# Mean of ReLU over rows: 126 rows a partition with two blocks of 128 rows, and a last row in pieces of 576, 192 and 256 columns

## The chip, the cores and the metric

One NeuronCore of a Trainium2 chip. The metric is the device time of one execution in microseconds (us); every run counted here was in the fast state at a granted clock of 1.00. ACT is ScalarE, DVE VectorE, POOL GpSimd, SP SyncE, which issues all transfers.

## The reference

```python
x: float32 [32, 512, 1024]           # 67.11 MB
return np.mean(np.maximum(x, 0), axis=-1)   # float32 [32, 512]
```

It is 16,384 rows of 1024 floats, each reduced to one float. Every byte of x is read once and used once.

## The kernel before

128 rows form a first block (one row a partition). The other 16,256 rows are laid out 127 consecutive rows a partition and read in tiles of 16 rows (8.39 MB, three buffers), then in pieces of 7, 4, 2 and 1 rows, and the last row in three column pieces.

```python
xfirst, xmain = xf[:P, :], xf[P:, :]
J = J - 1                                            # 127
xr = xmain.rearrange("(p j) d -> p j d", p=P, j=J)
NB, BUFS = 16, 3
row_pieces = [7, 4, 2, 1]
col_pieces = [512, 256, 256]
# ... SyncE issues the loads in order; each has its own semaphore
for t in range(full):
    buf_free(t)
    if t == 0:
        load(-1, row0[:, :], xfirst)
    load(t, bufs[t % BUFS][:, :, :], xr[:, t * NB:(t + 1) * NB, :])
# ... then row_pieces and col_pieces
# compute: even rows of a partition on ACT, odd ones on DVE, each with an accumulator
done = (dve_row if j % 2 else act_row)(nc, xt[:, k, :], sums[:, j:j + 1])
# ... the end, on the last row (n_done counts the signals so far):
nc.scalar.wait_ge(loaded[i + 1], 16)
act_row(nc, last[:, :512], last[:, D:D + 1]).then_inc(act, 1)
nc.vector.wait_ge(loaded[i + 2], 16)
dve_row(nc, last[:, 512:768], last[:, D + 1:D + 2]).then_inc(dve, 1)
nc.vector.wait_ge(act, n_done + 1)
nc.vector.wait_ge(dve, n_done + 1)
nc.vector.wait_ge(loaded[i + 3], 16)
nc.vector.scalar_tensor_tensor(                      # the final operation: takes the last 256
    out=last[:, 768:], in0=last[:, 768:], scalar=0.0,  # columns and both partial sums
    in1=scale[:, :], op0=ALU.max, op1=ALU.mult, accum_out=res[:, J - 1:J],
).then_inc(dve, 1)
nc.sync.wait_ge(pool, 2)
nc.sync.wait_ge(dve, n_done + 2)
nc.sync.dma_start(out=outr, in_=res[:, :]).then_inc(stored, 16)
```

The two partial sums sit in two columns behind the 256 data columns, so the final operation reads 258 elements. In the builds an instruction carries one wait of its own, and further waits are put into a separate semaphore instruction ahead of it.

Of the kernel before, what the change touches and what calls it, by code (L numbers as in the profile page):

```python
# [9 lines left out]
ACT = mybir.ActivationFunctionType  # L10


def act_row(nc, src, acc):

    return nc.scalar.activation(out=src, in_=src, func=ACT.Relu, accum_out=acc)  # L15


def dve_row(nc, src, acc, init=None):

    return nc.vector.tensor_scalar(  # L20
        out=src, in0=src, scalar1=0.0, scalar2=init,
        op0=ALU.max, op1=ALU.add, accum_out=acc,
    )


def issue_ahead_of_entry_barrier(nc, n):


    entry = nc.cur_f.blocks[0].instructions
    for _ in range(n):  # L30
        body, load = next(
            (block.instructions, k)
            for block in nc.cur_f.blocks[1:]
            for k, ins in enumerate(block.instructions)
            if ins.opcode == "DMACopy"
        )
        first = body[load]
        assert first.engine == mybir.EngineType.SP and not first.sync_info.on_wait
        assert all(i.opcode in ("Drain", "EventSemaphore") or i.engine != first.engine for i in body[:load])
        del body[load]  # L40
        at = next(k for k, i in enumerate(entry) if i.engine == first.engine and i.opcode == "Drain")
        entry.insert(at, first)


@with_exitstack
def kernel(
    ctx: ExitStack,
    tc: tile.TileContext,
    x: bass.AP,
    out: bass.AP,  # L50
):


    tc.close()
    tc.compile()  # L55

    nc = tc.nc
    P = nc.NUM_PARTITIONS
    xf = x.flatten_outer_dims()
    R, D = xf.shape  # L60
    assert R % P == 0
    J = R // P
    inv = 1.0 / D

    xfirst, xmain = xf[:P, :], xf[P:, :]
    outfirst, outmain = out.flatten()[:P], out.flatten()[P:]
    J = J - 1
    xr = xmain.rearrange("(p j) d -> p j d", p=P, j=J)
    outr = outmain.rearrange("(p j) -> p j", p=P, j=J)

    NB = 16
    BUFS = 3
    full = J // NB

    row_pieces = [7, 4, 2, 1]
    assert full * NB + sum(row_pieces) + 1 == J
    col_pieces = [512, 256, 256]
    assert sum(col_pieces) == D

    def sbuf(name, *shape):  # L80
        return ctx.enter_context(nc.sbuf_tensor(name, list(shape), F32))

    bufs = [sbuf(f"rows{b}", P, NB, D) for b in range(BUFS)]
    sums, res, part = sbuf("sums", P, J), sbuf("res", P, J), sbuf("part", P, 2)


    last = sbuf("last", P, D + 2)
    scale = sbuf("scale", P, D // 4 + 2)

    row0, mean0, turned0 = sbuf("row0", P, D), sbuf("mean0", P, 32), sbuf("turned0", P, 32)  # L90


    loaded = [nc.alloc_semaphore(f"loaded{i}") for i in range(full + len(row_pieces) + len(col_pieces) + 1)]
    act, dve, pool = (nc.alloc_semaphore(n) for n in ("act", "dve", "pool"))
    first = nc.alloc_semaphore("first")
    stored = nc.alloc_semaphore("stored")



    hinted = (nc.scalar, nc.vector)  # L100
    flag = nc.alloc_registers("flag", engines=[e.engine for e in hinted])
    nc.regs_mov(flag, 1)
    nc.br("rows_begin", engines=mybir.ALL_ENGINES)
    body = ctx.enter_context(nc.body("rows_begin", valid_engines=mybir.ALL_ENGINES))
    hints = [e.mark_branch_hint_location() for e in hinted]


    def load(i, dst, src):
        nc.sync.dma_start(out=dst, in_=src).then_inc(loaded[i], 16)

    def buf_free(t):

        if t >= BUFS:
            nc.sync.wait_ge(act, t - BUFS + 1)
            nc.sync.wait_ge(dve, t - BUFS + 1)

    for t in range(full):
        buf_free(t)
        if t == 0:
            load(-1, row0[:, :], xfirst)  # L120
        load(t, bufs[t % BUFS][:, :, :], xr[:, t * NB:(t + 1) * NB, :])
        if t == BUFS:

            nc.sync.wait_ge(first, 2)
            nc.sync.dma_start(
                out=outfirst.rearrange("(q i) -> q i", i=32), in_=turned0[0:P:32, :],
            ).then_inc(stored, 16)
    j0 = full * NB
    buf_free(full)
    xt = bufs[full % BUFS]  # L130
    lo, i = 0, full
    for n in row_pieces:
        load(i, xt[:, lo:lo + n, :], xr[:, j0 + lo:j0 + lo + n, :])
        lo, i = lo + n, i + 1
    c = 0
    for w in col_pieces:
        load(i, last[:, c:c + w], xr[:, J - 1, c:c + w])
        c, i = c + w, i + 1


    nc.gpsimd.memset(mean0[:, :], 0.0)  # L141
    nc.gpsimd.memset(scale[:, :], inv).then_inc(pool, 1)  # L142

    def rows(i, xt, lo, n, j0):
        nc.scalar.wait_ge(loaded[i], 16)
        nc.vector.wait_ge(loaded[i], 16)
        for k in range(lo, lo + n):
            j = j0 + k
            done = (dve_row if j % 2 else act_row)(nc, xt[:, k, :], sums[:, j:j + 1])
            if k >= lo + n - 2:  # L150
                done.then_inc(dve if j % 2 else act, 1)

    def finish(after, lo, hi):

        nc.gpsimd.wait_ge(act, after)
        nc.gpsimd.wait_ge(dve, after)
        nc.gpsimd.tensor_scalar(  # L157
            out=res[:, lo:hi], in0=sums[:, lo:hi], scalar1=inv, scalar2=0.0, op0=ALU.mult, op1=ALU.add,
        )

    nc.scalar.wait_ge(pool, 1)
    nc.vector.wait_ge(pool, 1)
    nc.scalar.wait_ge(loaded[-1], 16)
    nc.scalar.activation(  # L164
        out=row0[:, :], in_=row0[:, :], func=ACT.Relu, scale=inv, accum_out=mean0[:, 0:1],
    ).then_inc(first, 1)
    nc.vector.wait_ge(first, 1)
    nc.vector.transpose(turned0[:, :], mean0[:, :]).then_inc(first, 1)  # L168
    for t in range(full):
        rows(t, bufs[t % BUFS], 0, NB, t * NB)  # L170
    finish(full, 0, j0)
    lo, i = 0, full
    for n in row_pieces[:-1]:
        rows(i, xt, lo, n, j0)
        lo, i = lo + n, i + 1
    finish(i, j0, j0 + lo)


    prev = xt[:, lo, :]
    nc.scalar.wait_ge(loaded[i], 16)  # L180
    act_row(nc, prev[:, :448], part[:, 0:1]).then_inc(act, 1)
    nc.vector.wait_ge(loaded[i], 16)
    dve_row(nc, prev[:, 448:], part[:, 1:2]).then_inc(dve, 1)
    n_done = i + 1
    nc.gpsimd.wait_ge(act, n_done)
    nc.gpsimd.wait_ge(dve, n_done)
    nc.gpsimd.tensor_scalar(  # L187
        out=res[:, J - 2:J - 1], in0=part[:, 0:1], scalar1=part[:, 1:2], scalar2=inv, op0=ALU.add, op1=ALU.mult,
    ).then_inc(pool, 1)
    nc.scalar.wait_ge(loaded[i + 1], 16)  # L190
    act_row(nc, last[:, :512], last[:, D:D + 1]).then_inc(act, 1)
    nc.vector.wait_ge(loaded[i + 2], 16)
    dve_row(nc, last[:, 512:768], last[:, D + 1:D + 2]).then_inc(dve, 1)
    nc.vector.wait_ge(act, n_done + 1)
    nc.vector.wait_ge(dve, n_done + 1)
    nc.vector.wait_ge(loaded[i + 3], 16)
    nc.vector.scalar_tensor_tensor(  # L197
        out=last[:, 768:], in0=last[:, 768:], scalar=0.0, in1=scale[:, :], op0=ALU.max, op1=ALU.mult,
        accum_out=res[:, J - 1:J],
    ).then_inc(dve, 1)  # L200


    nc.sync.wait_ge(pool, 2)
    nc.sync.wait_ge(dve, n_done + 2)
    nc.sync.dma_start(out=outr, in_=res[:, :]).then_inc(stored, 16)

    used = [s.num for s in (*loaded, act, dve, pool, first)]
    assert used == list(range(used[0], used[0] + len(used)))
    nc.sync.sem_clear(range(used[0], used[-1] + 1))
    nc.sync.wait_ge(stored, 32).then_inc(stored, -32)  # L210

    for e, hint in zip(hinted, hints):
        e.br_lt(flag, 1, on_true="rows_begin", on_false="rows_end").branch_hint(hint)
    nc.br("rows_end", engines=[e for e in mybir.ALL_ENGINES if e not in (h.engine for h in hinted)])
    nc.switch_bb("rows_end")

    issue_ahead_of_entry_barrier(nc, 2)
# [30 lines left out]
```

## Time and profile before

| what | before |
|---|---|
| time, median of the first 3 runs (lowest to highest) | 161.46 us (161.40 to 161.55) |
| span of the profile | 160.2 us |
| DVE / ACT busy | 46% / 44% |
| DMA queue's share of 16 engines | 97.7% |
| last load complete, by the trace's semaphore records | 157.82 us |
| final store issued / complete | 158.57 / 160.21 us |

The lines are in the prediction. Read them in this order: busy shares (no engine is full, so something else sets the time), the DMA queue's share (it is full), the table of stretches (the rate is even), and last the timeline of the end, the only place where compute is not hidden by loads.

### The profile page before, as it was taken

How to read it: one execution, taken by the hardware profiler on the slowest of the kernel's cores; microseconds unless marked ns; L12 is line 12 of the kernel's file. 1: busy time of each engine (PE TensorE's matmuls, PEld its weight loads, DVE VectorE, ACT ScalarE, POOL GpSimd, SP SyncE). 2: the span in 40 equal slices, each digit the busy share in tenths (PEclk: the TensorE clock that was granted, in tenths of full speed). 3: DMA queues.
4: the chain of work that ended last, by engine and by line, in shares of the span. 5: the costliest groups of instructions: out<-in, count | busy, mean ns of one | idle time of the engine just before them, and what ended most of it. 6: DMA issues, size and time to landing. Idle time of an engine off the chain costs nothing. (4 is left out here: it accounts for less than half of the span.)

```text
span 160.2 us, 347 instructions
## 1 busy us (share of the span) xinstructions
DVE 73.3 (46%) x131; ACT 70.4 (44%) x133; POOL 1.3 (1%) x9
## 2 busy tenths in 40 slices
DVE  0000029900498006960079500993009920299984
ACT  1400029800496006950079300991009900299983
POOL 1000000000000000000000000000000000000001
DMA  9969969979989899699699699699699797998992
GB/s 393 507 278 523 507 278 523 442 344 523 409 376 523 360 425 524 294 491 523 262 524 523 262 523 524 262 523 523 262 524 458 327 523 327 425 451 367 419 412 102
DMA packets 2312, 67.18 MB, mean 419 GB/s; under 512 B 392, under 2 KB 648, under 8 KB 1032
## 3 DMA queue, kind: packets, MB, share of 16 engines
q1 hardware_dynamic: 2312, 67.18, 97.7%
HBM read 67.11 MB, written 0.07 MB: 419 GB/s over the span
## 5 line engine op out<-in xcount | busy, mean ns | idle before, releaser
L20 DVE TENSOR_SCALAR_CACHE_REDUCE rows<-rows 128x1024 f32<-128x1024 f32 (+1 forms) x63 | 72.1, 1208 | 78.9 <-DMA rows<-in_x_dram 78.7
L15 ACT ACTIVATE rows<-rows 128x1024 f32<-128x1024 f32 x64 | 66.2, 1035 | 84.1 <-DMA rows<-in_x_dram 83.9
L15 ACT ACTIVATION_READ_ACCUMULATOR rows<-rows 128x1 f32 x64 | 11.9, 186 | 0.0
L20 DVE DVE_READ_ACCUMULATOR rows<-rows 128x1 f32 x63 | 5.2, 82 | 0.0
L168 DVE STREAM_TRANSPOSE turned<-mean 128x32 f32<-128x32 f32 x1 | 0.2, 213 | 5.9 <-ACT row L164 5.9
L164 ACT ACT_TABLE_LOAD x1 | 1.3, 1283 | 3.3 <-DMA row<-in_x_dram 3.3
L157 POOL TENSOR_SCALAR res<-sums 128x112 f32<-128x112 f32 (+1 forms) x2 | 0.5, 250 | 154.0 <-DVE rows L20 154.0
L164 ACT ACTIVATE row<-row 128x1024 f32<-128x1024 f32 x1 | 1.1, 1056 | 0.0
L15 ACT ACTIVATE last<-last 128x512 f32<-128x512 f32 x1 | 0.6, 630 | 0.0
L20 DVE TENSOR_SCALAR_CACHE_REDUCE last<-last 128x256 f32<-128x256 f32 x1 | 0.4, 420 | 0.3 <-DMA last<-in_x_dram 0.3
L197 DVE SCALAR_TENSOR_TENSOR last<-last,scale 128x258 f32<-128x258 f32 x1 | 0.4, 428 | 0.1
L142 POOL MEMSET scale<- 128x258 f32 x1 | 0.3, 314 | 0.0
L187 POOL TENSOR_SCALAR res<-part 128x1 f32<-128x1 f32 x1 | 0.3, 267 | 0.6 <-DVE rows L20 0.6
L164 ACT ACTIVATION_READ_ACCUMULATOR row<-row 128x1 f32 x1 | 0.2, 186 | 0.0
L15 ACT ACTIVATION_READ_ACCUMULATOR last<-last 128x1 f32 x1 | 0.2, 186 | 0.0
L141 POOL MEMSET mean<- 128x32 f32 x1 | 0.1, 126 | 1.5 <-POOLq L55 1.5
L232 POOL MEMSET const-uint8-127<- 128x1 uint8 x1 | 0.1, 103 | 0.0
L232 POOL MEMSET const-bfloat16-1.0<- 128x1 bf16 x1 | 0.1, 102 | 0.0
L232 POOL MEMSET const-float32-0.0<- 128x1 f32 x1 | 0.1, 99 | 0.2 <-issue 0.2
L232 POOL MEMSET const-float32-1.0<- 128x1 f32 x1 | 0.1, 99 | 0.0
L20 DVE DVE_READ_ACCUMULATOR last<-last 128x1 f32 x1 | 0.1, 83 | 0.0
L197 DVE DVE_READ_ACCUMULATOR last<-last,scale 128x1 f32 x1 | 0.1, 82 | 0.0
## 6 DMA issues: line engine op xcount, KB each, us to landing
rows<-in_x_dram SPq DMA_DIRECT2D x1, 3584.0 KB, 38.1
rows<-in_x_dram SPq DMA_DIRECT2D x1, 2048.0 KB, 42.6
rows<-in_x_dram SPq DMA_DIRECT2D x1, 1024.0 KB, 44.7
row<-in_x_dram SPq DMA_DIRECT2D x1, 512.0 KB, 3.3
rows<-in_x_dram SPq DMA_DIRECT2D x1, 512.0 KB, 45.4
last<-in_x_dram SPq DMA_DIRECT2D x1, 256.0 KB, 45.6
last<-in_x_dram SPq DMA_DIRECT2D x2, 128.0 KB, 45.4
rows<-in_x_dram SPq DMA_DIRECT2D x7, 48.8
```

The lines of the kernel that those rows point to most:

```text
L15: return nc.scalar.activation(out=src, in_=src, func=ACT.Relu, accum_out=acc)
L20: return nc.vector.tensor_scalar(out=src, in0=src, scalar1=0.0, scalar2=init, op0=ALU.max, op1=ALU.add, accum_out=acc,)
L141: nc.gpsimd.memset(mean0[:, :], 0.0)
L142: nc.gpsimd.memset(scale[:, :], inv).then_inc(pool, 1)
L157: nc.gpsimd.tensor_scalar(out=res[:, lo:hi], in0=sums[:, lo:hi], scalar1=inv, scalar2=0.0, op0=ALU.mult, op1=ALU.add,)
L164: nc.scalar.activation(out=row0[:, :], in_=row0[:, :], func=ACT.Relu, scale=inv, accum_out=mean0[:, 0:1],).then_inc(first, 1)
L168: nc.vector.transpose(turned0[:, :], mean0[:, :]).then_inc(first, 1)
L187: nc.gpsimd.tensor_scalar(out=res[:, J - 2:J - 1], in0=part[:, 0:1], scalar1=part[:, 1:2], scalar2=inv, op0=ALU.add, op1=ALU.mult,).then_i ...
L197: nc.vector.scalar_tensor_tensor(out=last[:, 768:], in0=last[:, 768:], scalar=0.0, in1=scale[:, :], op0=ALU.max, op1=ALU.mult, accum_out=r ...
L232: nc = _bacc.Bacc("TRN2", target_bir_lowering=False, num_devices=1)
```

## The change

The intent: another layout of the main rows, a second small block, and a shorter chain between the last landing and the store. A third partial sum lets DVE share the first column piece with ACT, and the waits are reordered so that the signal expected last is written last. The core of the diff:

```diff
-    xfirst, xmain = xf[:P, :], xf[P:, :]
-    J = J - 1
+    xfirst, xmain = xf[:2 * P, :].rearrange("(c p) d -> p c d", c=2), xf[2 * P:, :]
+    J = J - 2
-    row_pieces = [7, 4, 2, 1]
+    row_pieces = [6, 4, 2, 1]
-    col_pieces = [512, 256, 256]
+    col_pieces = [576, 192, 256]
...
-        if t == 0:
-            load(-1, row0[:, :], xfirst)
+        if t in (0, 2):
+            c = t // 2
+            load(c - 2, row0[:, c, :], xfirst[:, c, :])
... (the second block's work on ACT goes ahead of tile 2, its store behind tile 5's load)
-    act_row(nc, last[:, :512], last[:, D:D + 1]).then_inc(act, 1)
+    act_row(nc, last[:, :448], last[:, D:D + 1]).then_inc(act, 1)
+    nc.vector.wait_ge(loaded[i + 1], 16)
+    dve_row(nc, last[:, 448:576], last[:, D + 1:D + 2])
     nc.vector.wait_ge(loaded[i + 2], 16)
-    dve_row(nc, last[:, 512:768], last[:, D + 1:D + 2]).then_inc(dve, 1)
-    nc.vector.wait_ge(act, n_done + 1)
+    dve_row(nc, last[:, 576:768], last[:, D + 2:D + 3]).then_inc(dve, 1)
     nc.vector.wait_ge(dve, n_done + 1)
     nc.vector.wait_ge(loaded[i + 3], 16)
+    nc.vector.wait_ge(act, n_done + 1)
...
+    nc.sync.wait_ge(dve, n_done + 2)
     nc.sync.wait_ge(pool, 2)
-    nc.sync.wait_ge(dve, n_done + 2)
```

More of the change, by code (lines that the diff above doesn't have):

```diff
@@ L63 @@
     inv = 1.0 / D
-    xfirst, xmain = xf[:P, :], xf[P:, :]
-    outfirst, outmain = out.flatten()[:P], out.flatten()[P:]
-    J = J - 1
+    xfirst, xmain = xf[:2 * P, :].rearrange("(c p) d -> p c d", c=2), xf[2 * P:, :]
+    outfirst, outmain = out.flatten()[:2 * P], out.flatten()[2 * P:]
+    J = J - 2
     xr = xmain.rearrange("(p j) d -> p j d", p=P, j=J)
@@ L84 @@
     sums, res, part = sbuf("sums", P, J), sbuf("res", P, J), sbuf("part", P, 2)
-    last = sbuf("last", P, D + 2)
-    scale = sbuf("scale", P, D // 4 + 2)
-    row0, mean0, turned0 = sbuf("row0", P, D), sbuf("mean0", P, 32), sbuf("turned0", P, 32)
-    loaded = [nc.alloc_semaphore(f"loaded{i}") for i in range(full + len(row_pieces) + len(col_pieces) + 1)]
+    last = sbuf("last", P, D + 3)
+    scale = sbuf("scale", P, D // 4 + 3)
+    row0, mean0, turned0 = sbuf("row0", P, 2, D), sbuf("mean0", P, 32), sbuf("turned0", P, 32)
+    loaded = [nc.alloc_semaphore(f"loaded{i}") for i in range(full + len(row_pieces) + len(col_pieces) + 2)]
     act, dve, pool = (nc.alloc_semaphore(n) for n in ("act", "dve", "pool"))
@@ L118 @@
         buf_free(t)
-        if t == 0:
-            load(-1, row0[:, :], xfirst)
+        if t in (0, 2):
+            c = t // 2
+            load(c - 2, row0[:, c, :], xfirst[:, c, :])
         load(t, bufs[t % BUFS][:, :, :], xr[:, t * NB:(t + 1) * NB, :])
-        if t == BUFS:
+        if t == BUFS + 2:
             nc.sync.wait_ge(first, 2)
-            nc.sync.dma_start(
-                out=outfirst.rearrange("(q i) -> q i", i=32), in_=turned0[0:P:32, :],
-            ).then_inc(stored, 16)
+            for c in range(2):
+                nc.sync.dma_start(
+                    out=outfirst[c * P:(c + 1) * P].rearrange("(q i) -> q i", i=32), in_=turned0[c:P:32, :],
+                ).then_inc(stored, 16)
     j0 = full * NB
@@ L162 @@
     nc.vector.wait_ge(pool, 1)
-    nc.scalar.wait_ge(loaded[-1], 16)
-    nc.scalar.activation(
-        out=row0[:, :], in_=row0[:, :], func=ACT.Relu, scale=inv, accum_out=mean0[:, 0:1],
-    ).then_inc(first, 1)
-    nc.vector.wait_ge(first, 1)
-    nc.vector.transpose(turned0[:, :], mean0[:, :]).then_inc(first, 1)
-    for t in range(full):
+    for t in range(full):
+        if t in (0, 2):
+            c = t // 2
+            nc.scalar.wait_ge(loaded[c - 2], 16)
+            done = nc.scalar.activation(
+                out=row0[:, c, :], in_=row0[:, c, :], func=ACT.Relu, scale=inv, accum_out=mean0[:, c:c + 1],
+            )
+            if c == 1:
+                done.then_inc(first, 1)
+                nc.vector.wait_ge(first, 1)
+                nc.vector.transpose(turned0[:, :], mean0[:, :]).then_inc(first, 1)
         rows(t, bufs[t % BUFS], 0, NB, t * NB)
@@ L209 @@
     nc.sync.sem_clear(range(used[0], used[-1] + 1))
-    nc.sync.wait_ge(stored, 32).then_inc(stored, -32)
+    nc.sync.wait_ge(stored, 48).then_inc(stored, -48)
     for e, hint in zip(hinted, hints):
```

## The prediction

> **What bounds the kernel now.** The kernel reads 32 x 512 x 1024 floats, 67.11 MB, reduces each row of 1024 to one number on ScalarE (ACT) or VectorE (DVE), and writes 65 KB. I read the page first: engine shares, DMA summary, costliest groups.
>
> ```profile
> DVE 73.3 (46%) x131; ACT 70.4 (44%) x133; POOL 1.3 (1%) x9
> DMA packets 2312, 67.18 MB, mean 419 GB/s; under 512 B 392, under 2 KB 648, under 8 KB 1032
> q1 hardware_dynamic: 2312, 67.18, 97.7%
> L20 DVE TENSOR_SCALAR_CACHE_REDUCE rows<-rows 128x1024 f32<-128x1024 f32 (+1 forms) x63 | 72.1, 1208 | 78.9 <-DMA rows<-in_x_dram 78.7
> L15 ACT ACTIVATE rows<-rows 128x1024 f32<-128x1024 f32 x64 | 66.2, 1035 | 84.1 <-DMA rows<-in_x_dram 83.9
> ```
>
> Both compute engines are idle more than half of the time, and nearly all of that idle time ends with a landing of input. The one queue keeps the 16 DMA engines busy for 97.7% of the span. Next I asked for the table by stretches, cut where tiles land, to see whether the DMA rate dips anywhere that a schedule could mend.
>
> ```profile
> core 0: us, DVE busy (x) ACT busy (x) POOL busy (x), PEclk, DMA share, GB/s
> 22.95:61.67 38.72, 18.41 (x32) 16.85 (x32) 0.00 (x0) 1.00 1.00 433
> 61.67:100.38 38.71, 18.41 (x32) 16.85 (x32) 0.00 (x0) 1.00 1.00 433
> ```
>
> Two tiles of 8.39 MB take 38.7 us at a DMA share of 1.00: 433 GB/s, with no hole. Last, the timeline of the end, because that is the only place where compute can still matter.
>
> ```profile
> 156.49 0.75 DVE L20 TENSOR_SCALAR_CACHE_REDUCE rows<-rows 128x576 f32<-128x576 f32 x1
> 157.16 0.63 ACT L15 ACTIVATE last<-last 128x512 f32<-128x512 f32 x1
> 157.54 0.42 DVE L20 TENSOR_SCALAR_CACHE_REDUCE last<-last 128x256 f32<-128x256 f32 x1 [0.29 <-DMA last<-in_x_dram]
> 157.70 0.19 ACT L15 ACTIVATION_READ_ACCUMULATOR last<-last 128x1 f32 x1
> 157.89 0.08 DVE L20 DVE_READ_ACCUMULATOR last<-last 128x1 f32 x1
> 158.06 0.43 DVE L197 SCALAR_TENSOR_TENSOR last<-last,scale 128x258 f32<-128x258 f32 x1
> 158.41 0.08 DVE L197 DVE_READ_ACCUMULATOR last<-last,scale 128x1 f32 x1
> 158.57 0.35 SPq L205 DMA_DIRECT2D out_dram<-res  x1
> ```
>
> The trace's semaphore records give what the timeline does not print: the three column pieces of the last row are complete at 157.14, 157.52 and 157.82 us; the accumulators signal at 157.90 (ACT) and 157.98 (DVE); the store is complete at 160.21. So the span of 160.2 is: 1.03 us before the first packet starts; about 156.8 us of gap-free stream until 157.82; 0.24 us from the last landing to the start of the final operation; 0.51 us for it and the store's issue; 1.64 us for the store to land. The measured 161.46 us has 1.3 us outside the span, which I leave as it is.
>
> **What the Trainium skill says.** "DMA: Bandwidth & Descriptors", section "Where 436 GB/s comes from", gives 435.2 GB/s as the most that 16 engines can take into SBUF. The 433 GB/s above agrees: the stream runs within 0.5% of that. The same page, "Latency and other measured facts", row on HBM row pitch, reports that a per-partition pitch of 512 KiB gave 207 GB/s in its copies against 214 unhindered. The pitch here is 127 x 4 KiB = 508 KiB before and 126 x 4 KiB = 504 KiB after. No stretch of this trace shows such a loss at 508; nothing shows 504 yet. "ScalarE: Activation LUTs", "What ACT_TABLE_LOAD costs", puts an ACTIVATE with immediate operands at 186 ns + 0.833 ns an element: 1039 ns for 1024, where the by-shape groups have 1042, and 559 for 448, where they have 577. I use the trace's 577.
>
> **The change part by part.**
>
> (1) *Bytes and packets.* All bytes of x are still read once. The packet records have medians of 159 ns for 4096 B, 1062 for 28,672 B and 2420 for 65,536 B, on each engine. The slope is (2420 - 159) / 61,440 = 0.0368 ns a byte, and 159 - 4096 x 0.0368 = 8 ns is left as the cost of a packet. A second block of 128 rows is one more transfer of 128 packets, 8 on each of 16 engines: 8 x 8 = 66 ns, and 9 ns for its 4-byte semaphore packet. The tile of 7 rows becomes 6, the three column pieces stay three: no change in packet count. The stream gets +0.08 us, so the last piece lands at about 157.90 instead of 157.82, if the rate stays.
>
> (2) *The second block's work.* One ACT row of 1.06 us + 0.19 us (minus overlap) in front of tile 2, in place of a row elsewhere. It lands about 1.3 us after tile 1, near 43.5, while ACT works on tile 1 until near 51 and then sits idle about 10.9 us before tile 2. Off the path. The transpose of 0.21 us moves behind the second block, and its stores behind tile 5's load: one more store of 4 packets of 13 ns. About zero.
>
> (3) *Landing of the last full tile.* The second block goes ahead of it: 524,288 B at 433 GB/s is 1.21 us, plus 0.08, so tile 6 lands at 140.57 rather than 139.28, with 14 rows behind it instead of 15. DVE takes a row every 1.14 us (139.30 to 140.44): before, 8 + 3 rows until 151.92 and then a wait of 0.79 us. After: 140.59 + 11 x 1.14 = 153.13, when the four-row piece (152.69 + 0.08 = 152.77) has already landed. DVE is 0.36 us late there; two rows bring it to 155.41 against a landing at 155.26, one more to 156.55 against a landing at 156.55. The debt is gone just there. Then the 576 part of the last but one row: 156.57 + 0.67 = 157.24. ACT is quicker (1.04 us a row) and never late.
>
> (4) *The last row.* Piece sizes go from 512, 256, 256 columns to 576, 192, 256. Packets of 768 B take 8 + 28 = 37 ns, so the 192 piece is 8 x 37 + 9 = 0.30 us; the last one took 0.30 (157.52 to 157.82). The 576 piece lands at 157.90 - 0.60 = 157.30 and the 192 piece at 157.60. ACT takes 448 columns: from 157.32, 0.577 us, accumulator signalled at 158.00 (before: 0.735 us after the start for 512; now 0.68). DVE takes 128 columns from 157.32, about 0.29 us by the slope between its 576 (754 ns) and 256 (420 ns), 1.04 ns an element, its accumulator read overlapping the next by 0.08; then 192 columns from 157.62, 0.35 us, signalled at 157.99. Before, the final operation started 0.08 us after the last of its signals (157.98 to 158.06); after: 158.00 + 0.08 = 158.08. That is 0.18 us behind the last landing instead of 0.24: a gain of 0.06 against the stream's loss of 0.08.
>
> (5) *Order of the waits.* The built program shows that the last operation's own wait is now DVE's, with the other two in a semaphore instruction ahead of it, and that SyncE now waits for the pool in the separate instruction and for DVE on the store itself. Before, DVE's signal at 158.51 passed a separate wait of 17 ns starting at 158.52 before the store started at 158.57. I credit 0.04 us.
>
> *Sum:* +0.08 (stream) - 0.06 (tail) - 0.04 (store's wait) = -0.02 us. The predicted time is 161.44 us.
>
> **The rivals.** *First: the pitch sets another HBM rate.* Summed over the trace, packets took 0.93 us an engine above the medians of their sizes, some 0.3 of it in the first packets. About 0.6 us are therefore scattered stalls in the stream, a few dozen 65,536 B packets at 2450 to 2650 ns, in clusters near 76, 87, 110 and 131 us. If those are partitions colliding in HBM, another pitch may remove them (161.44 - 0.6 = 160.8) or double them (162.0). 504 KiB is no power of two either; a loss of the 3% that the page gives for 512 KiB (161.4 x 1.03 = 166) needs a collapse for which the trace has no sign. *Second: DVE's debt from (3) reaches the end.* My slack is 0.02 us before the 576 part, 0.06 before the 128 part and 0.08 before the 192 part, 0.16 us together; if the last tile lands 0.2 us later than I say, the end moves by some 0.05: 161.5. *Third: the extra wait on a chain of three partial sums takes the place of the one removed.* If the 128 part's accumulator cannot overlap the next operation, DVE would still be idle at 157.60. No effect. *Fourth: the added stores disturb the stream.* The one store of before was queued behind tile 2 and ended at 81.21, and tiles 1 to 3 landed 19.37, 19.36 and 19.35 us apart; against.
>
> **Range and chances.** The bytes at 433 GB/s take 155 us of the 161.4; startup and the final store are not touched. To be faster by 2% the change would have to save 3.2 us, more than the 0.93 us of slow packets and the 0.75 us between last landing and the store's issue together. To be slower by 2% the stream would have to fall to 425 GB/s. I put 8 in 10 on 160.95 to 161.95: the packet stalls moving by their own size either way, and the usual spread of 0.15. Faster by over 2%: 0.01. Within 2%: 0.96. Slower: 0.03, nearly all of it for the pitch.
>
> **What would show each step right or wrong.** (1) The DMA queue's time stays at 97 to 98% of the span, the tile landings 19.35 to 19.5 us apart. (2) ACT's wait ahead of tile 2 some 0.3 us longer or shorter, no more: the block adds 1.29 us of stream and 1.15 of work. (3) The wait of 0.79 us on DVE before the four-row piece is gone, and tile 6 starts near 140.6. (4) The final operation starts near 158.08, 0.18 behind the last landing. (5) The store is issued within 0.03 us of DVE's signal. If tiles land 19.5 us apart or more from the start, the pitch was the change's real content and I have sized it wrongly; if the last landing is where I say but the store is late, the tail is.

## The result, and the profile after

The changed kernel took 161.59 us (median of 6 runs, 161.47 to 161.85) against 161.43 us (6 runs, 161.26 to 161.78) for the kernel before. The ratio is 1.0009, with a 95% interval of 0.9996 to 1.0022: no difference that these runs can see. A ratio here is always the mean time of one kernel's fast runs over the mean time of the other's fast runs of the same rounds, so it is not quite the ratio of the medians quoted beside it.

The page of the changed kernel, engine and DMA lines, and its table of stretches (window, length, busy time of DVE, ACT and POOL, granted clock, DMA share, GB/s):

```profile
DVE 73.3 (46%) x133; ACT 70.2 (44%) x133; POOL 1.3 (1%) x9
DMA packets 2464, 67.18 MB, mean 419 GB/s; under 512 B 416, under 2 KB 672, under 8 KB 1184
q1 hardware_dynamic: 2464, 67.18, 97.7%
```

```profile
62.97:101.70 38.73, 18.44 (x33) 16.88 (x33) 0.00 (x0) 1.00 1.00 433
```

There are 152 packets more, with the same bytes, the same share and the same 433 GB/s. The bound has not moved.

DVE's backlog ahead of the four-row piece: first the kernel before in its timeline (start, duration, instruction; in brackets the idle time before it and what ended it), then the changed kernel.

```profile
152.71 1.22 DVE L20 TENSOR_SCALAR_CACHE_REDUCE rows<-rows 128x1024 f32<-128x1024 f32 x1 [0.79 <-DMA rows<-in_x_dram]
```

```profile
152.50 1.06 ACT L15 ACTIVATE rows<-rows 128x1024 f32<-128x1024 f32 x1 [0.66 <-DMA rows<-in_x_dram]
...
152.85 1.21 DVE L20 TENSOR_SCALAR_CACHE_REDUCE rows<-rows 128x1024 f32<-128x1024 f32 x1
...
156.29 0.75 DVE L20 TENSOR_SCALAR_CACHE_REDUCE rows<-rows 128x576 f32<-128x576 f32 x1
```

DVE's wait of 0.79 us is gone. The piece landed at 152.48 and ACT began on it at once; DVE came 0.37 us late, still at work on the tile before. By 156.29 it is level again: that row landed at 156.26.

The end of the changed kernel, timeline and then the last steps of its chain of waits (start, duration, what; DVEq is DVE's sequencer, here the separate semaphore instruction):

```profile
157.05 0.58 ACT L15 ACTIVATE last<-last 128x448 f32<-128x448 f32 x1
157.05 0.29 DVE L20 TENSOR_SCALAR_CACHE_REDUCE last<-last 128x128 f32<-128x128 f32 x1
...
157.34 0.35 DVE L20 TENSOR_SCALAR_CACHE_REDUCE last<-last 128x192 f32<-128x192 f32 x1
157.53 0.19 ACT L15 ACTIVATION_READ_ACCUMULATOR last<-last 128x1 f32 x1
157.62 0.08 DVE L20 DVE_READ_ACCUMULATOR last<-last 128x1 f32 x1
157.85 0.43 DVE L205 SCALAR_TENSOR_TENSOR last<-last,scale 128x259 f32<-128x259 f32 x1
158.21 0.08 DVE L205 DVE_READ_ACCUMULATOR last<-last,scale 128x1 f32 x1
158.31 0.35 SPq L213 DMA_DIRECT2D out_dram<-res  x1
```

```profile
157.53 0.20 ACT last L15
157.73 0.03 issue
157.75 0.05 DVEq L204
157.81 0.04 issue
157.85 0.12 DVE last L205
```

Here the last load is complete at 157.63, ACT signals at 157.73, DVE at 157.72. The chain names ACT: its signal has to pass the separate semaphore instruction (0.03 + 0.05 + 0.04), so the final operation starts 0.12 us after it and 0.22 us after the last landing; before it was 0.24. The store follows the read of the accumulator within 0.03 us, where it took 0.07 before.

Two things in this first pair of profiles did not fit. The last load was complete 0.19 us earlier than before although packets were added, and the store needed 1.84 us to land instead of 1.64. The experiments had to say whether these are effects of the change or chance.

### The profile page after: what moved, and what is told of

Its sections match the earlier page's. It is cut to its first block, busy times and chain, and to the rows that moved or that the text cites. A ratio compares the mean times of both kernels' runs of the same rounds, so it can differ in the third digit from the quotient of the medians.

```text
span 160.2 us, 351 instructions
## 1 busy us (share of the span) xinstructions
DVE 73.3 (46%) x133; ACT 70.2 (44%) x133; POOL 1.3 (1%) x9
## 4 chain that ended last, share of the span: by engine, by line
DMA 73%; DVE 17%; another core or an unknown queue 6%; SPq 1%; issue 1%; ACT 0%; DVEq 0%
DMA rows<-in_x_dram 45%; DMA last<-in_x_dram 28%; DVE rows L20 17%; SPq L109 1%; ACT last L15 0%; DVE last L205 0%; DVEq L204 0%; SPq L115 0%; DVEq L148 0%
## 5 line engine op out<-in xcount | busy, mean ns | idle before, releaser
L15 ACT ACTIVATE rows<-rows 128x1024 f32<-128x1024 f32 (+1 forms) x63 | 65.2, 1035 | 84.0 <-DMA rows<-in_x_dram 83.9
L169 ACT ACTIVATE row<-row 128x1024 f32<-128x1024 f32 x2 | 2.1, 1048 | 0.0
L20 DVE TENSOR_SCALAR_CACHE_REDUCE last<-last 128x128 f32<-128x128 f32 (+1 forms) x2 | 0.6, 320 | 0.0
L15 ACT ACTIVATE last<-last 128x448 f32<-128x448 f32 x1 | 0.6, 576 | 0.1
```

The costliest lines, as they stand in the source:

```text
L15: return nc.scalar.activation(out=src, in_=src, func=ACT.Relu, accum_out=acc)
L20: return nc.vector.tensor_scalar(out=src, in0=src, scalar1=0.0, scalar2=init, op0=ALU.max, op1=ALU.add, accum_out=acc,)
L169: done = nc.scalar.activation(out=row0[:, c, :], in_=row0[:, c, :], func=ACT.Relu, scale=inv, accum_out=mean0[:, c:c + 1],)
```

## The experiments

Twelve runs were made, in three batches of four (on chips 5, 3 and 5); each is compared with runs of the kernel before in the same batch. Times are medians. Where a run has one execution more than it has rounds, its profiled execution is not in the ratio: the 162.16 us of *changed again* are left out of its 0.9987, and with them the means would give 161.33 / 161.37 = 0.9997.

| run | time, us | before, us | ratio (95%) | last landing | final operation behind it | store, issue to landing | stalls after 8 us |
|---|---|---|---|---|---|---|---|
| before, first profile | | | | 157.82 | 0.24 | 1.64 | 0.58 |
| changed, first profile | 161.59 | 161.43 | 1.0009 (0.9996 to 1.0022) | 157.63 | 0.22 | 1.84 | 0.28 |
| pitch 512 KiB | 161.44 | 161.42 | 0.9997 (0.9983 to 1.0011) | 157.74 | 0.22 | 1.61 | 0.35 |
| pitch 508 KiB | 161.31 | 161.42 | 0.9993 (0.9979 to 1.0007) | 157.72 | 0.24 | 1.62 | 0.27 |
| blocks only | 161.31 | 161.42 | 0.9992 (0.9978 to 1.0005) | 157.46 | 0.22 | 1.61 | 0.27 |
| tail only | 161.34 | 161.42 | 0.9995 (0.9981 to 1.0009) | 157.67 | 0.24 | 1.59 | 0.23 |
| before again | 161.31 | 161.34 | 0.9999 (0.9986 to 1.0013) | 157.52 | 0.24 | 1.58 | 0.24 |
| changed again | 161.16 | 161.34 | 0.9987 (0.9973 to 1.0000) | 158.45 | 0.25 | 1.61 | 1.26 |
| quarter transfers | 162.74 | 161.34 | 1.0089 (1.0073 to 1.0104) | 159.07 | 0.23 | 1.58 | |
| DVE late | 162.04 | 161.34 | 1.0040 (1.0025 to 1.0056) | 157.55 | 1.06 | 1.62 | 0.27 |
| waits only | 161.63 | 161.47 | 0.9997 (0.9982 to 1.0012) | 158.15 | 0.25 | 1.67 | 0.38 |
| ACT's own wait | 161.58 | 161.47 | 1.0007 (0.9990 to 1.0025) | 158.40 | 0.19 | 1.83 | 1.07 |
| straight | 161.91 | 161.47 | 1.0019 (1.0006 to 1.0033) | 158.39 | 0.31 | 1.53 | 0.37 |
| straight, split store | 161.86 | 161.47 | 1.0018 (1.0005 to 1.0031) | 158.69 | 0.27 | 1.42 | 0.61 |

The four columns on the right are of the one profiled execution of each. Stalls are what packets took above the median of their size, summed and divided by the 16 engines, without the start-up of the first 8 us; all in us. (For the quarter transfers the sum mixes stalls with other packet sizes and is left out.)

### Is the row pitch at work?

```diff
-    xr = xmain.rearrange("(p j) d -> p j d", p=P, j=J)          # 504 KiB from partition to partition
+    xr = xf.rearrange("(p j) d -> p j d", p=P)[:, :J, :]         # run "pitch512"
+    xr = xf[P:, :].rearrange("(p j) d -> p j d", p=P)[:, :J, :]  # run "pitch508"
```

Both read partly other rows than the results are stored for, so both are wrong (relative error 0.064); the traffic has the same size and shape.

> The changed kernel with one edit: the main loads start every partition 512 KiB behind the one before it instead of 504 (the first 126 of each 128 rows are read, so the results are wrong on purpose; packets, bytes and work are the same). My theory, that the DMA engines and not the HBM side set the rate of this stream: the same time as the changed kernel within 0.3 us, tiles 19.35 to 19.5 us apart, ratio to the kernel before 0.999 to 1.003. The rival, that the pitch moves the HBM rate, with the size that the skill's page has for 512 KiB (207 against 214 GB/s): tiles near 20 us apart and 165 to 166.5 us.

> The changed kernel with its main loads at the pitch of the kernel before, 508 KiB (126 of each 127 rows; results wrong on purpose), all else the same. My theory: 161.4 to 161.7 us, no different from the changed kernel. The rival, that the smaller sum of slow packets in the changed kernel's profile (0.71 us an engine against 0.93) comes from the 504 KiB pitch: 0.2 us slower than the changed kernel, and the clusters of 2450 to 2650 ns packets after 120 us are back.

The table of stretches at 512 KiB:

```profile
62.97:101.70 38.73, 18.41 (x32) 16.85 (x32) 0.00 (x0) 1.00 1.00 433
```

It is the line of the 504 KiB kernel but for two short instructions. The ratios to the kernel before are 0.9997 and 0.9993. No effect of the pitch is seen in this stream (the intervals reach from 0.9979 to 1.0011), and a 3% loss is excluded. My rival's account of the stalls finds no support either: at 508 KiB they are 0.27 us, as at 504 and 512, and not the 0.58 of the first profile; the second profile of the kernel before, below, settles that.

### Each half alone

*Blocks only* is the changed kernel with the end of the kernel before put back. *Tail only* is the kernel before with the three column pieces, the third partial sum and the order of the waits of the changed kernel (the diffs are the two halves of the diff above).

> Only the first half of the change: 126 rows and two blocks of 128 rows, with the column pieces, the two partial sums and the order of the waits of the kernel before. My theory: 0.08 us of packets are added and nothing is gained, so 161.5 us, ratio 1.0005 (0.999 to 1.002), with the final operation 0.22 to 0.26 us behind the last landing as before. The rival, that DVE's debt reaches the end: the final operation 0.3 us or more behind the last landing, ratio above 1.001.

> Only the second half: 127 rows and one block as before, with the pieces of 576, 192 and 256 columns, three partial sums and the new order of the waits. My theory: the final operation starts 0.18 to 0.22 us behind the last landing (0.24 before), and the store starts 0.02 us behind DVE's signal (0.06 before): 0.06 to 0.1 us less, ratio 0.9995 (0.998 to 1.001). The rival, that the store's own landing takes back what is gained: store started earlier by 0.1 us behind the last landing, landing of the store 1.7 us or more after its start instead of 1.64, ratio 1.000 or above.

Neither half shows a cost or a gain in the times (0.9992 and 0.9995, both intervals contain 1). The profiles separate what the times cannot. The end with blocks only, then with the tail only:

```profile
157.51 0.08 DVE L20 DVE_READ_ACCUMULATOR last<-last 128x1 f32 x1
157.69 0.43 DVE L203 SCALAR_TENSOR_TENSOR last<-last,scale 128x258 f32<-128x258 f32 x1
158.04 0.08 DVE L203 DVE_READ_ACCUMULATOR last<-last,scale 128x1 f32 x1
158.19 0.35 SPq L211 DMA_DIRECT2D out_dram<-res  x1
```

```profile
157.59 0.19 ACT L15 ACTIVATION_READ_ACCUMULATOR last<-last 128x1 f32 x1
157.64 0.08 DVE L20 DVE_READ_ACCUMULATOR last<-last 128x1 f32 x1
157.91 0.43 DVE L199 SCALAR_TENSOR_TENSOR last<-last,scale 128x259 f32<-128x259 f32 x1 [0.18 <-ACT last L15]
158.26 0.08 DVE L199 DVE_READ_ACCUMULATOR last<-last,scale 128x1 f32 x1
158.37 0.35 SPq L207 DMA_DIRECT2D out_dram<-res  x1
```

Old end: the accumulator is read by 158.12, the store starts 0.07 us later. New end: read by 158.34, the store 0.03 later. That 0.05 us repeats in every profile: 0.03 in all with the new order on SyncE, 0.07 in all three with the old one. The final operation itself did not move: 0.24 us behind the last landing with the tail only, where I had expected 0.18 to 0.22. The new wait (the 0.18 us in brackets) is on ACT.

### Which oddities were chance

*Before again* and *changed again* are unedited.

> The kernel before, unedited, as a control with a second profile. My theory, that the stalls in the stream (packets slower than the median of their size, 0.58 us an engine after the first 8 us in its first profile) are chance: ratio 1.000 within 0.001, and a sum of such stalls as the kernels of the first four experiments had, 0.2 to 0.35 us, with the last landing near 157.6. The rival, that they belong to this kernel: 0.5 us or more again and the last landing near 157.8.

> The changed kernel, unedited, once more. My theory: ratio 0.999 to 1.001, and the final store lands 1.6 us after its start as in all profiles but one, so that the 1.84 us of its first profile was chance. The rival, that the change makes the store slower: 1.8 us again, ratio 1.0005 to 1.0015.

The first two rows are from the second profile of the kernel before, the third from that of the changed kernel (one fence each):

```profile
61.67:100.38 38.71, 18.41 (x33) 16.85 (x33) 0.00 (x0) 1.00 1.00 433
100.38:139.28 38.90, 18.61 (x33) 17.05 (x33) 0.00 (x0) 1.00 0.97 418
```

```profile
101.76:141.16 39.40, 18.41 (x32) 16.85 (x32) 0.00 (x0) 1.00 0.96 409
```

The second profile of the kernel before has its last landing at 157.52 and 0.24 us of stalls, so 157.82 and 0.58 were not properties of that kernel. The profiled execution of the changed kernel happened to be its slow one (162.16 us; its other five took 161.11 to 161.23): two tiles took 39.40 us between 101.76 and 141.16, where two tiles take 38.7, and the last landing came at 158.45. *ACT's own wait*, below, had two runs of 162.25 and 162.26; the profiled one shows such stalls too (1.07 us). These stalls come and go between executions of one kernel (0.28 and 1.26 us in the changed one, its last landing 0.8 us apart) and are larger than everything that this change does. The store's 1.84 us is no property of the kernel either: 1.61 here, and once more 1.83 with *ACT's own wait*; what makes it so in two of fourteen profiles, no run shows. The two ratios of the changed kernel, 1.0009 and 0.9987 (0.9997 with the run of 162.16), lie on both sides of 1.

### What a packet costs

```diff
-        load(t, bufs[t % BUFS][:, :, :], xr[:, t * NB:(t + 1) * NB, :])
+        for q in range(0, NB, 4):
+            load(t, bufs[t % BUFS][:, q:q + 4, :], xr[:, t * NB + q:t * NB + q + 4, :])
```

(The waits on a full tile go from 16 to 64.)

> The changed kernel with each full tile loaded by four transfers of 4 rows instead of one of 16: packets of 16,384 B instead of 65,536 B, the same bytes. By the 8 ns a packet of my sum: 168 packets more on each engine are 1.4 us, and 21 semaphore packets of 9 ns 0.2 us: 163.1 us, ratio 1.010. The rival, that the cost of a packet is hidden behind its neighbours: within 0.2 us of the changed kernel.

```profile
DMA packets 5488, 67.18 MB, mean 416 GB/s; under 512 B 752, under 2 KB 1008, under 8 KB 1520
q1 hardware_dynamic: 5488, 67.18, 98.3%
```

The ratio to the kernel before is 1.0089 (1.0104 at most). The edit was made to the changed kernel, though, and against that one on the same chip the median is 162.74 - 161.16 = 1.58 us longer, where my sum had 1.6. The landings say the same without the chance of the start. From landing to landing, two full tiles take:

```profile
63.42:102.57 39.15, 18.41 (x32) 16.85 (x32) 0.00 (x0) 1.00 1.01 428
```

The same two tiles of the changed kernel landed 38.70 us apart (62.88 to 101.58). The 0.45 us are 48 more packets on each engine and 6 semaphore packets of 9 ns: (450 - 54) / 48 = 8 ns a packet, as predicted. (The medians are too coarse for this: four packets of 612 ns are 30 ns more than one of 2418, four of 611, the median in most other profiles, 26; that is 10 or 9 ns for each of three more packets.) Note how it is hidden in the busy share: the queue is *busier* (98.3%) and slower. The cost of a packet adds up and is not hidden. The second block's own cost shows in the landings too: it lands 1.27 us after tile 1 and pushes everything behind it back, and the six-row piece takes 7.30 us where the seven-row one took 8.52. The net is 0.05 us, where my sum had 0.08; in the times it cannot be seen.

### How much slack DVE has

```diff
+        if t == full - 1:
+            extra = sbuf("extra", P, 1)
+            nc.vector.wait_ge(loaded[t], 16)
+            dve_row(nc, row0[:, 0, :], extra[:, :])
```

> The changed kernel with one more row of 1.14 us for DVE ahead of its last full tile (it reads the first block again into a spare sum; the result is right). By my account of the end DVE has 0.16 us of slack there, so the final operation starts about 1.0 us later behind the last landing (1.2 us instead of 0.22) and the time is 162.5 us, ratio 1.006. The rival, that DVE's debt has room because ACT and the last landing set the end: under 0.3 us more.

```profile
158.48 0.09 DVE L20 DVE_READ_ACCUMULATOR last<-last 128x1 f32 x1
158.60 0.43 DVE L209 SCALAR_TENSOR_TENSOR last<-last,scale 128x259 f32<-128x259 f32 x1
```

The load was complete at 157.55, the final operation started 1.06 us later: 0.84 us more than in the first profile of the changed kernel, of 1.14 us added. Against the changed kernel on the same chip the median is 0.88 us longer (162.04 against 161.16; I had expected 162.5). So DVE had 0.30 us of room, not 0.16. It has two parts: DVE's own signal moved by 0.93 us (its waits for data had held 0.21), and the final operation now starts 0.03 us after that signal instead of 0.12 after ACT's, because DVE's signal is the one that the instruction itself waits for. It is the only profile in which that signal comes last by far.

### The place of a wait

```diff
 # "waits_only": the kernel before, with only the new order
-    nc.vector.wait_ge(act, n_done + 1)
     nc.vector.wait_ge(dve, n_done + 1)
     nc.vector.wait_ge(loaded[i + 3], 16)
+    nc.vector.wait_ge(act, n_done + 1)
...
-    nc.sync.wait_ge(pool, 2)
     nc.sync.wait_ge(dve, n_done + 2)
+    nc.sync.wait_ge(pool, 2)
 # "act_own": the changed kernel, with the old order on DVE
+    nc.vector.wait_ge(act, n_done + 1)
     nc.vector.wait_ge(dve, n_done + 1)
     nc.vector.wait_ge(loaded[i + 3], 16)
-    nc.vector.wait_ge(act, n_done + 1)
```

The built programs show that the wait written first stays with the instruction and the others go into the separate one: written (act, dve, loaded), the operation itself waits for ACT, and the separate instruction for the load and then DVE; written (dve, loaded, act), the operation waits for DVE, and the separate instruction for ACT and then the load.

> The kernel before with nothing but the new order of the waits, on DVE ahead of the final operation and on SyncE ahead of the store. By the runs so far, a signal that the instruction itself waits for releases it in 0.03 us, one that a separate semaphore instruction waits for in 0.08 to 0.12 us. So: the store starts 0.02 to 0.03 us behind DVE's read of the accumulator (0.07 before), the final operation starts 0.20 us behind the last landing (0.24 before), together 0.09 us: ratio 0.9994 (0.998 to 1.001), to be seen in the profile and hardly in the times. The rival, that the order of the waits changes nothing: 0.24 and 0.07.

> The changed kernel with its three waits ahead of the final operation written in the order of the kernel before, so that ACT's signal, the last to come, is the one that the operation itself waits for. My theory, that the change put the last signal behind the separate instruction and lost there what the smaller ACT share won: the final operation 0.16 to 0.18 us behind the last landing instead of 0.22 to 0.25. The rival, that the place of the wait is indifferent: 0.22 to 0.25 again. Ratio 0.999 to 1.001 in both, too little for the times.

On SyncE the order is worth what I said: 0.03 us behind the accumulator in place of 0.07. On DVE, *waits only* missed: 0.25 us, not 0.20. There the last load's signal was at 158.15 and ACT's at 158.27, 0.12 later and not the 0.08 I had taken from the first profile, and it passed the separate instruction in another 0.12. *ACT's own wait* gave 0.19 us, better than the 0.22 to 0.25 of the changed kernel and short of the expected 0.16 to 0.18:

```profile
158.31 0.19 ACT L15 ACTIVATION_READ_ACCUMULATOR last<-last 128x1 f32 x1
158.41 0.08 DVE L20 DVE_READ_ACCUMULATOR last<-last 128x1 f32 x1
158.59 0.43 DVE L205 SCALAR_TENSOR_TENSOR last<-last,scale 128x259 f32<-128x259 f32 x1
```

Both engines signal at 158.51 here, so now DVE's signal is the one that passes the separate instruction, in 0.08 us. The change's intent, the last signal last, was turned round by the build; undoing it is worth 0.03 to 0.06 us in this one profile, far below what the times resolve (1.0007, 0.9990 to 1.0025).

The price of the separate instruction is no scatter. By the semaphore records it is 0.08 us in all four profiles in which DVE's signal comes last there, as the second of its two waits (both profiles of the kernel before, *blocks only*, *ACT's own wait*), and 0.12 us in all nine in which ACT's comes last, as the first of the two. The place in the pair and the engine that signals changed together in every kernel, so which of them makes the 0.04 us was not isolated.

### A version without blocks

```diff
-    xfirst, xmain = ...two blocks of 128 rows
-    J = J - 2
+    xr = xf.rearrange("(p j) d -> p j d", p=P, j=J)      # J = 128, first load is tile 0
-    row_pieces = [6, 4, 2, 1]
+    row_pieces = [8, 4, 2, 1]
-    col_pieces = [576, 192, 256]
+    col_pieces = [640, 192, 192]                          # ACT 416 columns, DVE 224
 # "straight_split" besides: the first 112 sums of a partition are stored before the end
+    nc.sync.wait_ge(pool, 2)
+    nc.sync.dma_start(out=outr[:, :j0], in_=res[:, :j0]).then_inc(stored, 16)
```

> The version to which the runs point: 128 rows a partition and no block of 128 rows at all, since the pitch costs nothing and each block costs 8 packets an engine; column pieces 640, 192 and 192 with 416 columns for ACT, so that the final operation has 192 columns; the new order of the waits. Against the kernel before: 0.08 us of packets less, final operation 0.36 us instead of 0.43 and started 0.20 us behind the last landing instead of 0.24, store's wait 0.05 less: 0.24 us in all, ratio 0.9985 (0.997 to 1.000). The rival, that stalls of the stream, some 0.2 to 0.9 us by chance, cover all of it: no ratio below 0.9995.

> The same with the first 112 sums of each partition stored early, behind the last loads, so that the final store has 16 sums, 64 B a partition instead of 512. Its 8 packets an engine take 9 or 10 ns instead of 27: 0.14 us less from the store's start to its landing, 1.45 us instead of 1.6, ratio 0.9976 (0.996 to 0.999). The rival, that the landing is round trip and not data, or waits for the early store's: 1.55 us or more, no better than the version without the split.

Both results are correct, and both kernels are slower than the kernel before: 1.0019 (1.0006 to 1.0033) and 1.0018. I had expected 0.9985 and 0.9976, so I had missed something. The loads show it. The GB/s line of the page (40 slices of the span) starts, for the version without blocks, and then for the changed kernel:

```profile
GB/s 261 522 424 359 522 424 359 522 424 359 522 359 424 522 359 424 522 359 424 522 326 457 522 310 473 522 310 473 489 326 489 489 326 489 375 424 408 410 407 81
```

```profile
GB/s 393 507 278 524 507 278 524 442 344 524 393 524 262 524 524 262 524 524 262 524 475 311 524 425 360 524 376 409 524 262 524 524 262 524 360 430 421 411 409 80
```

A packet is counted in the slice where it starts, so the swing between 262 and 524 is only the rhythm of large packets; the first slice is the point. In the packet records of the version without blocks the 16 engines start their first packet, of 65,536 B, between 1.03 and 2.39 us, and that packet takes 2.7 to 3.3 us instead of 2.42. In the first profile of the kernel before the first 16 packets start between 1.03 and 1.39 us. With a block first, the first packets have 4096 B, and all 16 engines have completed the whole first block within 0.5 us of one another, by 3.3 us in the changed kernel. The skew of the start stays to the end: without blocks the 16 completions of the first tile spread over 0.97 us and those of the last load over 0.90 (157.49 to 158.39), with the split store over 1.02. In the changed kernel it is 0.35 (157.28 to 157.63), and in the twelve profiles with a block first 0.28 to 0.53, but for one where a stall at tile 3 pulled the engines apart to 0.80. The mean of the 16 is later too, 157.89 against 157.44, and the last one counts. So the block at the front seems to be worth several tenths of a microsecond: it lets all engines begin together. That it is the size of the first transfer, and not something else that the version without blocks changed, was not isolated. The second block has no such task.

The rest of the version did what it could. The store took 1.53 us with 512 B a partition and 1.42 us with the split (1.45 expected); the final operation took 0.36 us. But its start was 0.31 and 0.27 us behind the last landing instead of 0.20: the first column piece landed only 0.49 and 0.52 us ahead of the last one there, not 0.60, and ACT and DVE were late with it.

No version that I ran beats the kernel before beyond the noise. One that keeps a single block first, with the new order on SyncE and ACT's signal on the operation's own wait, would by my estimate from these profiles (0.05 on SyncE, 0.03 to 0.06 on DVE) gain about 0.1 us; it was not run, and 0.1 us is within the interval of any of these comparisons.

## Why the prediction was right or wrong

The time was right: 161.44 predicted, 161.59 and 161.16 measured in two batches, ratios 1.0009 and 0.9987 against a predicted 0.9999. The reason was right too: the stream of loads ran at 433 GB/s before and after, none of the edits touches it by more than the cost of its packets, and what was won at the end is under 0.1 us. How near the number came is partly luck. In the first profile the last landing was 0.27 us earlier than predicted and the store took 0.20 longer, neither of them the change's doing by the later profiles, and the two nearly cancel; the predicted -0.02 us itself is far below what the times can show.

- **(1) Bytes and packets: right in size, wrong in its base.** The packet's cost of 8 ns is shown by the quarter transfers; the block's net cost was 0.05 us by the landings, 0.08 in my sum. The landing at 157.90 was not met (157.63), because I added the 0.08 us to a profile with 0.58 us of stalls. From the second profile of the kernel before, 157.52, it is 0.11 us later, but *blocks only*, with the same block, landed at 157.46. I had seen those stalls and still took one execution for the base.
- **(2) The second block's work: right.** It is off the path: ACT's wait ahead of tile 2 went from 10.94 to 11.16 us (some 0.3 either way predicted), and *blocks only* has ratio 0.9992.
- **(3) DVE's debt: right.** It was predicted to be 0.36 us late at the four-row piece and was 0.37, and level at the last but one row (0.02 us late predicted; 0.03 behind the landing measured, as in any unhindered start). The slack behind it was mis-sized: 0.30 us by the late-DVE run, 0.16 in my sum. The waits for data held 0.21 of it; the other 0.09 is that a late DVE's signal starts the operation in 0.03 us and ACT's in 0.12, which I had taken as equal.
- **(4) The last row: half right.** ACT and DVE signalled 0.10 and 0.09 us behind the last landing, as worked out (0.10 and 0.09). The term that failed is the 0.08 in "after: 158.00 + 0.08 = 158.08": I carried it from DVE's signal in the kernel before over to ACT's, though I had read in the built program that the places of the waits were exchanged. ACT's signal took 0.12, here and in the eight other profiles in which it comes last in the separate instruction. That is the whole miss of the first profile: 0.18 + 0.04 = 0.22. The gain was 0.02 us at best, and none in the tail-only and the second profile, instead of 0.06.
- **(5) Order of the waits on SyncE: right.** 0.05 us, credited with 0.04.
- **The rivals.** The pitch was given most of the chance of a slower result and shows no effect at 504, 508 or 512 KiB. The stalls I wanted to tie to it move between executions of the same kernel. The added stores left no mark: full tiles land 19.35 to 19.37 us apart in the changed kernel (the one behind the second block apart), behind the stores too. (The one store of before was queued behind tile 3, which landed at 81.03, not behind tile 2; the spacings that I gave as those of tiles 1 to 3 are those of tiles 2 to 4.)

## What to carry to other kernels

When the DMA queue is at 97 to 98% of the span and at an even rate, first work out the most that can be won outside the stream; here it was about 2.4 us of end and 1 us of start, and an edit that moves 0.05 us of that cannot be seen in times that vary by 0.3 to 0.5. Repeat the profile of the kernel before as well as that of the change before reading a difference of tenths between two traces. If several waits guard one instruction, look in the built program which of them the instruction itself carries, and give that place to the signal that comes last.

## What the Trainium skill lacked or had wrong

- "DMA: Bandwidth & Descriptors", "Latency and other measured facts", row on HBM row pitch: its loss at a pitch of 512 KiB (207 against 214 GB/s, in copies between HBM tensors) is not seen for these loads into SBUF with 64 KiB packets: ratio 0.9997 to the kernel at 508 KiB, 433 GB/s at 504 and 512. The row says what it was measured on; whether the direction or the packet size makes the difference was not tested.
- No page that I read has the start of the 16 engines: with first packets of 65,536 B the engines started over 1.36 and 1.23 us in two profiles and completed the last load over 0.90 and 1.02 us; with a first block in packets of 4096 B the last completions lay within 0.28 to 0.53 us in eleven of twelve profiles.
- "DMA: Bandwidth & Descriptors", "Why small descriptors are slow (HBM only)", has a fixed overhead of about 3 cycles a packet, with no time in ns; these runs show 8 ns for each packet of 4 to 64 KiB, which adds up in full (1.58 us for 168 packets an engine and their semaphores).
- "Perfetto Trace Analysis", "Identifying Dependency Chains", says that separate semaphore instructions may be inserted ahead of an instruction with several waits, without a price: here 0.03 us from signal to start for the instruction's own wait (one profile), and through the separate one on DVE 0.08 us (four profiles, DVE's signal) or 0.12 us (nine, ACT's).
- No page that I read has the chance stalls in the stream: 0.23 to 1.26 us an engine after the start, by execution and not by kernel.
